# Squares of the sub-norm moved from a PSUM bank to an SBUF tile, and a priority for emptying the banks of transposed probabilities

## The chip, the cores and the metric

The kernel runs on one core of a Trainium2 chip. The metric is the device time of one execution in microseconds (us). The median of the three timed executions of the kernel before is 1237.96 us (1237.94 to 1243.18).

Names used below: PE is TensorE (PEld its weight load), ACT is ScalarE, DVE is VectorE, POOL is GpSimd, SP is the engine whose queue issues most DMAs. L663 is line 663 of the kernel before.

## The reference

Two layers work on 16 meta tokens and 1024 tokens of 1024 features. Each layer computes

```
h = RMSNorm(x)
[f_in | q | k | v | gate] = h @ W_in
Fourier part:   Re(FFT2 over positions and channels) per group, then a 128 x 128 map
Attention part: a = softmax(q0 k0) - lambda * softmax(q1 k1); o = a @ v   (4 heads, two maps each)
                o = RMSNorm(o) * gain                                     (the sub-norm, over the 128 values of a head)
x = x + (concat(Fourier, o) * silu(gate)) @ W_out
```

and the meta tokens are dropped at the end. All of it is float32 to a tolerance that one rounded pass doesn't meet.

## The kernel before

**Split products.** Matmuls take operands rounded to a shorter format (type fp32r). Each operand is split in two: a high part, the rounded copy, and a low part, the value less the high part. A product is then three matmuls (high by high, high by low, low by high). So whatever PE writes to PSUM and later uses as an operand is read out of its bank twice: ACT casts it to the high part, then DVE subtracts that from the bank to get the low part. The bank comes free when DVE is done.

**PSUM.** Three pools divide the eight banks: `big()` is one tile of three banks (S in the profile) for the scores of one softmax map; `gbank()` gives two single banks (G) for projections and output matmuls; `bank()` gives three single banks (M) for transposes and for the attention's products with v.

**Stages of a layer.** `fourier` projects and transforms the Fourier groups. `head_projection` then makes q, k, v and gate of head 0. After that `attention` runs over the 4 heads, in each over four groups of two row tiles of 128 queries, and feeds other work between its own matmuls: `fill` takes steps from the generator `rest`, which holds the projections of heads 1 to 3 (L547 on PE), then the two halves of the output product (L286 on PE).

**One item of attention** (one row tile of one head) is `scores`, then, one item later, `transposes`. In `scores`, for each of the two maps, PE makes 128 x 1040 scores in S (L635, L637), DVE negates them into SBUF and takes the row minimum (L642), ACT takes the exponential with its row sum (L645). DVE then forms the sum's ratio (L649, L651) and subtracts the second map from the first (L653). In `transposes`, PE transposes the resulting p in eight 128 x 128 blocks into two banks of M, four to a bank (L663). ACT copies each bank to `ath` (L667), DVE writes the low part to `atl` (L668). A third bank takes the 16 meta columns (L670), emptied by L673 and L674.

**End of a group.** When the last row tile of a group is transposed, `drain` first calls `flush_finish` for the group before it if that is still open, then `values` multiplies by v into a bank (L682, L683) and copies the result to `osb` (L685). `finish` is called between the next item's scores: SP loads the gate (L693), PE transposes `osb` into a bank of M (L696), ACT copies that back to SBUF (L698). ACT then takes, for each of the two row tiles, the squares of the SBUF copy with their row sum (L703). The squares themselves are not used; before the change they are written over the same bank of M, so the bank stays taken until the second square is done. DVE, POOL and DVE make the scale (L705, L707, L708), DVE applies it (L710), and SP stores the result (L712).

**What sets the order.** The program is traced in the order of the code and each instruction gets a priority from its place. A planner then runs the whole program in a simulated time of its own: on each engine it takes, of the instructions that are ready by that time, the one that comes first in priority; it gives out the buffers of a pool by the same simulated times. What it writes out is a fixed order for each engine with semaphore waits between engines. `tc.high_priority(EVAC)` with EVAC = 600 (L44) puts instructions 600 places ahead; before the change it is used for emptying the G and S banks of the projections (L432, L469) and of the output product (L292). `issue_after` keeps the fed work behind a mark of attention.

**Small tiles.** `sm` (L59) is an SBUF pool of three buffers for each tag. It holds among others `ssq`, `ms`, `rs` of `norm_tile` (L216 to L220), `ss` and `rsq` of the query and key norms (L490, L500), and `r1`, `so`, `rso` of `finish` (L699 to L706).

Of the kernel before, what the change touches and what calls it, by code (L numbers as in the profile page):

```python
# [10 lines left out]
F32 = mybir.dt.float32  # L11
F32R = mybir.dt.float32r
AF = mybir.ActivationFunctionType
ALU = mybir.AluOpType
# [4 lines left out]
P = 128  # L19
# [24 lines left out]
EVAC = 600  # L44
# [6 lines left out]
def trunk(ctx: ExitStack, tc, x, meta, ngain, w_in, w_f, qg, kg, lq1, lk1, lq2, lk2, subg, w_out,  # L51
          ident_d, chan_d, rope_d, dft_d, dftt_d, out, dbg=None):
    nc = tc.nc
    pe, act, dve, pool, sp = nc.tensor, nc.scalar, nc.vector, nc.gpsimd, nc.sync
# [4 lines left out]
    sm = ctx.enter_context(tc.tile_pool(name="sm", bufs=3))  # L59
# [7 lines left out]
    def nm(s):  # L67
        uid[0] += 1
        return f"{s}_{uid[0]}"
# [10 lines left out]
    def f(ap):  # L80
        return ap.bitcast(F32)
# [131 lines left out]
    def norm_tile(hT, hM, gb, xt, t, wk, inplace=False):  # L213
        R, pos = tile_rows(t), P * t
        xn = wk.tile([P, D], F32, tag="xn", name=nm("xn"), bufs=1 if inplace else 2)
        ssq = sm.tile([P, 1], F32, tag="ssq", name=nm("ssq"))  # L216
        act.activation(xn[0:R], xt[0:R], AF.Square, accum_out=ssq[0:R])
        ms = sm.tile([P, 1], F32, tag="ms", name=nm("ms"))
        dve.tensor_scalar(ms[0:R], ssq[0:R], 1.0 / D, EPS, op0=ALU.mult, op1=ALU.add)
        rs = sm.tile([P, 1], F32, tag="rs", name=nm("rs"))  # L220
        pool.tensor_tensor(rs[0:R], ms[0:R], nhalf[0:R, 0:1], op=ALU.pow)
        if inplace:
            xn = xt
        dve.scalar_tensor_tensor(xn[0:R], xt[0:R], rs[0:R], gb[0:R], op0=ALU.mult, op1=ALU.mult)
        for c in range(2):
            pb = bank()
            for j in range(4):
                k = 4 * c + j
                pe.transpose(pb[:, R * j:R * j + R], xn[0:R, P * k:P * k + P], ident[0:R, 0:R])
            src = pb[:, 0:4 * R].rearrange("p (k r) -> p k r", k=4)  # L230
            hi = hT[:, 4 * c:4 * c + 4, 0, pos:pos + R]
            lo = hT[:, 4 * c:4 * c + 4, 1, pos:pos + R]
            act.copy(hi, src)
            dve.tensor_tensor(lo, src, f(hi), op=ALU.subtract)
            if t == NT:
                for o, part in ((0, hi), (32, lo)):
                    act.copy(hM[:, 4 * c:4 * c + 4, o:o + R], f(part))
# [218 lines left out]
    def head_projection(li, h, hT, hM, ep, wk, store, w, nxt, progress):  # L456
        c = P * h
# [6 lines left out]
        ss = None  # L464

        def evacuate(t, ps, a, kv):
            nonlocal ss
            R = tile_rows(t)
            with tc.high_priority(EVAC):  # L469
                if t == NT:  # L470
                    pm = [ep.tile([P, 256], F32, tag="sq", name=nm("pm"), bufs=3) for _ in range(2)]
                    for part, u, v in ((pm[0], a, 256), (pm[1], 256, 384 if kv else 512)):
                        part = part[0:R, u % 256:(v - 1) % 256 + 1]
                        act.copy(part, ps[32:32 + R, u:v])
                        dve.tensor_tensor(part, ps[0:R, u:v], part, op=ALU.add)
                    pqk, pvg = pm[0], pm[1]
                else:
                    pqk, pvg = ps[:, 0:256], ps[:, 256:512]
                if not kv:
                    gs = ep.tile([P, P], F32, tag="gs", name=nm("gs"), bufs=2)  # L480
                    act.activation(gs[0:R], pvg[0:R, P:2 * P], AF.Tanh, scale=0.5)
                    dve.scalar_tensor_tensor(gs[0:R], gs[0:R], 1.0, pvg[0:R, P:2 * P], op0=ALU.add, op1=ALU.mult)
                act.copy(qk[0:R, t, a:256], pqk[0:R, a:256])
                sq = ep.tile([P, 256], F32, tag="sq", name=nm("sq"), bufs=3)
                act.activation(sq[0:R, a:256], pqk[0:R, a:256], AF.Square)
                act.copy(va[0:R, t, :], pvg[0:R, 0:P])
            if not kv:
                sp.dma_start(gtd[li][h][t, 0:R, :], gs[0:R])
            if t % 3 == 0:
                ss = sm.tile([P, 12], F32, tag="ss", name=nm("ss"))  # L490
            c0, c1 = 4 * (t % 3) + a // HD, 4 * (t % 3) + 4
            if t == NT:
                pool.memset(ss[:, 4 * (t % 3):c1], 1.0)
            dve.tensor_reduce(ss[0:R, c0:c1], sq[0:R, a:256].rearrange("p (c d) -> p c d", d=HD), axis=AX.X,
                              op=ALU.add)
            if t % 3 == 2:
                t0 = t - 2
                reg = qk[:, t0:t0 + 3, :]
                dve.tensor_scalar(ss, ss, 1.0 / HD, EPS, op0=ALU.mult, op1=ALU.add)  # L499
                rs = sm.tile([P, 12], F32, tag="rsq", name=nm("rsq"))  # L500
                pool.tensor_tensor(rs, ss, nhalf[:, 0:12], op=ALU.pow)  # L501
                n12 = reg.rearrange("p t (c d) -> p (t c) d", d=HD)
                dve.tensor_tensor(n12, n12, rs.unsqueeze(2).to_broadcast([P, 12, HD]), op=ALU.mult)
                n5 = reg.rearrange("p t (i c d) -> p (t i) c d", i=2, d=HD)

                def tab(x, lo, hi):
                    y = x[:, t0:t0 + 3, :, lo:hi].rearrange("p t i d -> p (t i) d")
                    return y.unsqueeze(2).to_broadcast([P, 6, 2, hi - lo])

                r1 = ep.tile([P, 256], F32, tag="sq", name=nm("r1"), bufs=3)  # L510
                r2 = ep.tile([P, 256], F32, tag="sq", name=nm("r2"), bufs=3)
                r1 = r1[:, 0:12 * ROT].rearrange("p (t c d) -> p t c d", t=6, c=2)
                r2 = r2[:, 0:12 * ROT].rearrange("p (t c d) -> p t c d", t=6, c=2)
                dve.tensor_tensor(r1, n5[:, :, :, 0:ROT], tab(cgt, 0, 16), op=ALU.mult)
                dve.tensor_tensor(r2[:, :, :, 0:8], n5[:, :, :, 8:16], tab(sgt, 0, 8), op=ALU.mult)
                dve.tensor_tensor(r2[:, :, :, 8:16], n5[:, :, :, 0:8], tab(sgt, 8, 16), op=ALU.mult)
                dve.tensor_tensor(n5[:, :, :, 0:ROT], r1, r2, op=ALU.add)
                progress[h] = t // 3 + 1
                if t == NT and ("qk", li, h) in dbg:
                    sp.dma_start(dbg["qk", li, h], qk)  # L520

        for group in [(t,) for t in range(NT - 1)] + [(NT - 1, NT)]:
# [14 lines left out]
            for k in range(KT):  # L537
                for t in group:
# [4 lines left out]
                    else:  # L543
                        hi, lo = hT[:, k, 0, pos:pos + P], hT[:, k, 1, pos:pos + P]
# [11 lines left out]
    def attention(li, wk, store, fill, marks, ready, progress):  # L556
        ath = wk.tile([P, NT, 272], F32R, name="ath", bufs=1)
        atl = wk.tile([P, NT, 272], F32R, name="atl", bufs=1)
# [97 lines left out]
        def transposes(pa, i, t):  # L656
            R = tile_rows(t)
            qo = P * i
            for c in range(2):
                pb = bank()  # L660
                for j in range(4):
                    kt = 4 * c + j
                    pe.transpose(pb[:, R * j:R * j + R], pa[0:R, P * kt:P * kt + P],  # L663
                                 ident[0:R, 0:R])
                src = pb[:, 0:4 * R].rearrange("p (j r) -> p j r", j=4)
                hi = ath[:, 4 * c:4 * c + 4, qo:qo + R]
                act.copy(hi, src)  # L667
                dve.tensor_tensor(atl[:, 4 * c:4 * c + 4, qo:qo + R], src, f(hi), op=ALU.subtract)  # L668
            pb = bank()
            ins = pe.transpose(pb[0:NMETA, 0:R], pa[0:R, SEQ:L], ident[0:R, 0:R])  # L670
            marks.append(ins.ins)
            for o in (0, 64):
                act.copy(att[o:o + NMETA, qo:qo + R], pb[0:NMETA, 0:R])  # L673
            dve.tensor_tensor(att[32:32 + NMETA, qo:qo + R], pb[0:NMETA, 0:R], f(att[0:NMETA, qo:qo + R]),  # L674
                              op=ALU.subtract)
# [12 lines left out]
        def finish(h, gi, osb, ls):  # L688
            sets = [(0, 2, P)] + ([(2, 1, NMETA)] if len(group_tiles(gi)) > 2 else [])
            for i0, n, R in sets:  # L690
# [3 lines left out]
                pb = bank()  # L694
                for i in range(n):
                    pe.transpose(pb[0:R, P * i:P * i + P], osb[:, P * (i0 + i):P * (i0 + i) + R], ident)  # L696
                ot = osb[:, 0:2 * P].rearrange("p (t d) -> p t d", t=2)
                act.copy(ot[0:R, 0:n], pb[0:R, 0:P * n].rearrange("p (t d) -> p t d", t=n))  # L698
                r1 = sm.tile([P, 2], F32, tag="r1", name=nm("r1"))  # L699
                dve.reciprocal(r1[0:R, 0:n], ls[0:R, i0:i0 + n])  # L700
                so = sm.tile([P, 2], F32, tag="so", name=nm("so"))
                for i in range(n):
                    act.activation(pb[0:R, P * i:P * i + P], ot[0:R, i], AF.Square, scale=r1[0:R, i:i + 1],  # L703
                                   accum_out=so[0:R, i:i + 1])
                dve.tensor_scalar(so[0:R, 0:n], so[0:R, 0:n], 1.0 / P, EPS, op0=ALU.mult, op1=ALU.add)  # L705
                rs = sm.tile([P, 2], F32, tag="rso", name=nm("rso"))  # L706
                pool.tensor_tensor(rs[0:R, 0:n], so[0:R, 0:n], nhalf[0:R, 0:n], op=ALU.pow)  # L707
                dve.tensor_tensor(rs[0:R, 0:n], rs[0:R, 0:n], r1[0:R, 0:n], op=ALU.mult)  # L708
                for i in range(n):
# [291 lines left out]
```

## Time and profile before

| | us |
|---|---|
| median of the three timed executions | 1237.96 |
| the profiled execution | 1239.06 |
| its span, from the first instruction to the last | 1236.9 |
| PE busy | 1169.6 |
| DVE busy | 832.9 |
| ACT busy | 647.4 |
| POOL busy | 262.8 |

The profile is of one execution. A row of a timeline reads: start and duration in us, engine, line, operation, what it writes and reads, how many instructions in a row are merged, and in brackets the idle time of the engine before it with what ended it. Matmuls are pipelined, so that a busy PE isn't PE at its peak. By the windows of the profile the first layer's attention lies at about 224 to 630 us, the second layer's at about 860 to 1198 us; the stages between are the Fourier parts, the first head's projections and the ends of the output products.

### The profile page before, as it was taken

How to read it: one execution, taken by the hardware profiler on the slowest of the kernel's cores; microseconds unless marked ns; L12 is line 12 of the kernel's file. 1: busy time of each engine (PE TensorE's matmuls, PEld its weight loads, DVE VectorE, ACT ScalarE, POOL GpSimd, SP SyncE). 2: the span in 40 equal slices, each digit the busy share in tenths (PEclk: the TensorE clock that was granted, in tenths of full speed). 3: DMA queues.
4: the chain of work that ended last, by engine and by line, in shares of the span. 5: the costliest groups of instructions: out<-in, count | busy, mean ns of one | idle time of the engine just before them, and what ended most of it. 6: DMA issues, size and time to landing. Idle time of an engine off the chain costs nothing.

```text
span 1236.9 us, 18756 instructions
## 1 busy us (share of the span) xinstructions
PE 1169.6 (95%) x6676; PEld 1000.8 (81%) x6676; DVE 832.9 (67%) x1793; ACT 647.4 (52%) x1588; POOL 262.8 (21%) x231
## 2 busy tenths in 40 slices
PE   6999899989998998999999999999999999999998
PEld 6999786877777776778879998877878887878786
DVE  6352435777778778887775244557768888898863
ACT  6232325566657667566453323344667666766631
POOL 5111216023212213011012103252142121211200
PEclk9999899999999999999999999999999999999999
DMA  7420203012002004644436111120020020265353
GB/s 227 136 69 35 73 27 99 7 30 75 12 18 82 16 25 147 187 148 130 147 113 197 54 34 55 59 80 26 16 82 22 28 73 25 82 225 162 109 162 114
DMA packets 103612, 105.46 MB, mean 85 GB/s; under 512 B 11232, under 2 KB 87584, under 8 KB 103264
## 3 DMA queue, kind: packets, MB, share of 16 engines
q1 hardware_dynamic: 103104, 99.59, 25.9%
q0 software_dynamic: 416, 4.70, 1.1%
q8 instruction: 52, 0.85, 0.3%
q14 instruction: 40, 0.33, 0.1%
HBM read 74.62 MB, written 29.62 MB: 84 GB/s over the span
## 4 chain that ended last, share of the span: by engine, by line
PE 66%; DVE 12%; DMA 7%; ACT 6%; issue 5%; POOL 2%; SPq 1%; POOLq 0%; ACTq 0%; DVEq 0%
PE G L547 20%; PE G L286 10%; PE G L352 7%; PE S L352 6%; PE M L682 5%; PE S L635 4%; PE S L637 3%; PE S L547 3%; DVE p L642 3%; PE M L663 2%; PE M L393 2%; DMA wst<-in_w_in_dram 2%; ACT p L645 2%; DVE p L653 1%; DMA xt<-in_x_dram 1%
## 5 line engine op out<-in xcount | busy, mean ns | idle before, releaser
L547 PE MATMUL G<-wh,hT 128*128 128x512 f32 x896 | 308.7, 404 | 4.7 <-ACT wh L182 2.5
L645 ACT ACTIVATE p<-p,mx 128x1040 f32<-128x1040 f32 x136 | 158.4, 1165 | 99.7 <-DVE p L642 96.6
L547 PEld LDWEIGHTS G<-wh,hT 128*128 128x128 f32 x896 | 169.2, 190 | 44.6 <-ACT wh L182 3.4
L642 DVE TENSOR_SCALAR_CACHE_REDUCE p<-S 128x1040 f32<-128x1040 f32 x136 | 167.8, 1234 | 33.0 <-PE S L637 28.4
L547 PE MATMUL G<-wl,hT 128*128 128x512 f32 x448 | 178.2, 399 | 1.8 <-POOL wl L184 1.8
L184 POOL TENSOR_TENSOR wl<-wst,wh 128x512 fp32r<-128x512 f32 x82 | 112.6, 1384 | 235.7 <-ACT wh L182 131.1
L286 PE MATMUL G<-wh,yh 128*128 128x512 f32 (+2 forms) x276 | 107.8, 404 | 3.6 <-DVE xt L293 2.3
L182 ACT CAST wh<-wst 128x512 fp32r<-128x512 f32 x128 | 75.0, 620 | 65.0 <-DMA wst<-in_w_in_dram 22.2
L286 PE MATMUL G<-wl,yh 128*128 128x512 f32 (+2 forms) x276 | 106.6, 395 | 0.0
L501 POOL TENSOR_TENSOR rsq<-ss,nhalf 128x12 f32<-128x12 f32 x24 | 58.4, 2433 | 219.4 <-DVE ss L499 190.8
L547 PEld LDWEIGHTS G<-wl,hT 128*128 128x128 f32 x448 | 85.3, 190 | 18.1 <-POOL wl L184 2.8
L352 PE MATMUL G<-hT,wh 128*128 128x384 f32 (+3 forms) x384 | 96.4, 332 | 0.0
L286 PE MATMUL G<-wh,yl 128*128 128x512 f32 (+1 forms) x260 | 93.4, 400 | 0.0
L668 DVE TENSOR_TENSOR atl<-M,ath 128x512 fp32r<-128x512 f32 x136 | 87.0, 656 | 8.0 <-ACT ath L667 6.9
L352 PE MATMUL S<-hT,wh 128*128 128x256 f32 (+3 forms) x384 | 90.7, 320 | 1.0 <-DVE sg L440 1.0
L653 DVE SCALAR_TENSOR_TENSOR p<-p,cc,p 128x1040 f32<-128x1040 f32 (+1 forms) x68 | 89.2, 1312 | 1.5
L637 PE MATMUL S<-k,ql 128*128 128x264 f32 (+3 forms) x408 | 87.3, 321 | 0.0
L667 ACT CAST ath<-M 128x512 fp32r<-128x512 f32 x136 | 73.8, 561 | 22.0 <-PE M L663 21.2
L707 POOL TENSOR_TENSOR rso<-so,nhalf 128x2 f32<-128x2 f32 (+1 forms) x36 | 25.3, 702 | 273.6 <-DVE so L705 256.5
L663 PE MATMUL M<-ident,p 128*128 128x128 f32 x544 | 74.2, 270 | 7.4 <-ACT M L703 3.5
L184 DVE TENSOR_TENSOR wl<-wst,wh 128x512 fp32r<-128x512 f32 x46 | 44.4, 966 | 47.6 <-ACT wh L182 47.3
L663 PEld LDWEIGHTS M<-ident,p 128*128 128x128 f32 x544 | 61.6, 140 | 15.4 <-ACT M L703 4.4
(193 smaller groups left out, 2542.1 us busy)
## 6 DMA issues: line engine op xcount, KB each, us to landing
wst<-in_w_in_dram SPq DMA_DIRECT2D x64, 192.0 KB, 2.8
xt<-in_x_dram SPq DMA_DIRECT2D x16, 512.0 KB, 3.9
wst<-in_w_in_dram SPq DMA_DIRECT2D x32, 256.0 KB, 3.6
wst<-in_w_out_dram SPq DMA_DIRECT2D x16, 512.0 KB, 4.0
xmid<-xt SPq DMA_DIRECT2D x16, 512.0 KB, 3.3
xt<-xmid SPq DMA_DIRECT2D x16, 512.0 KB, 4.3
tab<-in_dft_dram POOLq DMA_DIRECT2D x2, 2096.0 KB, 10.0
yfd<-sg SPq DMA_DIRECT2D x8, 520.0 KB, 2.7
```

What stands on the lines that cost most here:

```text
L182: act.copy(h, self.staged[q][:, j, :])
L184: eng.tensor_tensor(l, self.staged[q][:, j, :], f(h), op=ALU.subtract)
L286: pe.matmul(pb[0:m, 0:e - c], lhsT=a[:, k, 0:m], rhs=b[2 * k + n][:, c:e], start=k == 0 and i == 0, stop=k == 3 and i == n_pass - 1)
L352: pe.matmul(o, lhsT=w[k][:, c:c + P], rhs=hT[:, k, s, a:b], start=k == 0 and i == 0, stop=k == KT - 1 and i == 2)
L547: pe.matmul(pss[t][0:part.shape[-1], a:b], lhsT=part, rhs=w[k][:, a:b], start=k == 0 and i == 0, stop=k == KT - 1 and i == len(pairs) - 1)
L637: ins = pe.matmul(ps[0:R, C0 + a:C0 + b], lhsT=ql[:, qo:qo + R], rhs=kk[:, a:b], start=False, stop=True)
L642: dve.tensor_scalar(pc[0:R], ps[0:R, C0:C0 + L], -1.0, None, op0=ALU.mult, op1=ALU.min, accum_out=mx[0:R])
L645: act.activation(pc[0:R], pc[0:R], AF.Exp, bias=mx[0:R], scale=-1.0, accum_out=lc)
L653: dve.scalar_tensor_tensor(pp[0][0:R], pp[1][0:R], cc[0:R], pp[0][0:R], op0=ALU.mult, op1=ALU.add)
L663: pe.transpose(pb[:, R * j:R * j + R], pa[0:R, P * kt:P * kt + P], ident[0:R, 0:R])
L667: act.copy(hi, src)
L668: dve.tensor_tensor(atl[:, 4 * c:4 * c + 4, qo:qo + R], src, f(hi), op=ALU.subtract)
```

## The change

The squares of `finish` go to a new SBUF tile `sqo` of 128 x 128 with one buffer, in place of the bank of M; their row sums go where they went. L667 and L668 come under `tc.high_priority(EVAC)`. Seven small tags of `sm` get two buffers in place of three.

```diff
@@ norm_tile
-        ssq = sm.tile([P, 1], F32, tag="ssq", name=nm("ssq"))
+        ssq = sm.tile([P, 1], F32, tag="ssq", name=nm("ssq"), bufs=2)
         act.activation(xn[0:R], xt[0:R], AF.Square, accum_out=ssq[0:R])
-        ms = sm.tile([P, 1], F32, tag="ms", name=nm("ms"))
+        ms = sm.tile([P, 1], F32, tag="ms", name=nm("ms"), bufs=2)
         dve.tensor_scalar(ms[0:R], ssq[0:R], 1.0 / D, EPS, op0=ALU.mult, op1=ALU.add)
-        rs = sm.tile([P, 1], F32, tag="rs", name=nm("rs"))
+        rs = sm.tile([P, 1], F32, tag="rs", name=nm("rs"), bufs=2)
@@ head_projection
-                ss = sm.tile([P, 12], F32, tag="ss", name=nm("ss"))
+                ss = sm.tile([P, 12], F32, tag="ss", name=nm("ss"), bufs=2)
...
-                rs = sm.tile([P, 12], F32, tag="rsq", name=nm("rsq"))
+                rs = sm.tile([P, 12], F32, tag="rsq", name=nm("rsq"), bufs=2)
@@ transposes
                 hi = ath[:, 4 * c:4 * c + 4, qo:qo + R]
-                act.copy(hi, src)
-                dve.tensor_tensor(atl[:, 4 * c:4 * c + 4, qo:qo + R], src, f(hi), op=ALU.subtract)
+                with tc.high_priority(EVAC):
+                    act.copy(hi, src)
+                    dve.tensor_tensor(atl[:, 4 * c:4 * c + 4, qo:qo + R], src, f(hi), op=ALU.subtract)
@@ finish
-                so = sm.tile([P, 2], F32, tag="so", name=nm("so"))
+                so = sm.tile([P, 2], F32, tag="so", name=nm("so"), bufs=2)
+                sqo = wk.tile([P, P], F32, tag="sqo", name=nm("sqo"), bufs=1)
                 for i in range(n):
-                    act.activation(pb[0:R, P * i:P * i + P], ot[0:R, i], AF.Square, scale=r1[0:R, i:i + 1],
+                    act.activation(sqo[0:R], ot[0:R, i], AF.Square, scale=r1[0:R, i:i + 1],
                                    accum_out=so[0:R, i:i + 1])
...
-                rs = sm.tile([P, 2], F32, tag="rso", name=nm("rso"))
+                rs = sm.tile([P, 2], F32, tag="rso", name=nm("rso"), bufs=2)
```

## Rows read from the trace of the kernel before

**Rows 1.** The page: span, busy time by engine, the chain by engine.
```profile
span 1236.9 us, 18756 instructions
PE 1169.6 (95%) x6676; PEld 1000.8 (81%) x6676; DVE 832.9 (67%) x1793; ACT 647.4 (52%) x1588; POOL 262.8 (21%) x231
...
PE 66%; DVE 12%; DMA 7%; ACT 6%; issue 5%; POOL 2%; SPq 1%; POOLq 0%; ACTq 0%; DVEq 0%
```

**Rows 2.** Windows, by stage: window, length, PE, PEld, DVE, ACT, POOL, clock, DMA, GB/s.
```profile
224.00:480.00 256.00, 237.81 (x1355) 195.52 (x1354) 200.41 (x452) 165.18 (x413) 54.09 (x45) 0.99 0.13 36
860.00:1085.00 225.00, 218.08 (x1278) 185.59 (x1277) 181.03 (x405) 151.64 (x385) 50.98 (x40) 1.00 0.17 50
480.00:630.00 150.00, 142.36 (x808) 117.29 (x806) 119.41 (x248) 85.71 (x201) 20.38 (x21) 0.99 0.49 154
1085.00:1198.00 113.00, 109.75 (x634) 92.32 (x633) 98.16 (x197) 67.57 (x153) 14.29 (x13) 1.00 0.49 158
```

**Rows 3.** Waits of PE, whole span: released by; us in total, times, longest.
```profile
PE M L670 <- DVE atl L668: 9.5, 6, 3.2
PE M L670 <- ACT M L703: 9.3, 8, 2.0
PE S L635 <- DVE p L642: 4.5, 7, 1.4
PE M L663 <- ACT M L703: 3.5, 3, 1.7
...
PE M L682 <- DVE atl L668: 1.2, 2, 1.0
```

**Rows 4.** Timeline around one wait for the squares: ACT, then PE.
```profile
251.63 0.35 ACT L698 COPY osb<-M 128x256 f32<-128x256 f32 x1
251.89 1.07 ACT L667 CAST ath<-M 128x512 fp32r<-128x512 f32 x2
...
253.38 0.37 ACT L703 ACTIVATE M<-osb,r 128x128 f32<-128x128 f32 x1
...
251.88 0.64 PE L637 MATMUL S<-k,ql 128*128 128x264 f32 x3
253.93 0.28 PE L670 MATMUL M<-ident,p 128*16 128x128 f32 x1 [1.41 <-ACT M L703]
```

**Rows 5.** Timeline around the longest wait for L668, with a finish: ACT, DVE, PE.
```profile
273.48 0.37 ACT L698 COPY osb<-M 128x256 f32<-128x256 f32 x1
...
273.75 2.27 DVE L653 SCALAR_TENSOR_TENSOR p<-p,cc,p 128x1040 f32<-128x1040 f32 x1
276.05 1.29 DVE L668 TENSOR_TENSOR atl<-M,ath 128x512 fp32r<-128x512 f32 x2
...
276.80 0.29 PE L670 MATMUL M<-ident,p 128*16 128x128 f32 x1 [3.17 <-DVE atl L668]
```

**Rows 6.** Timeline around a wait for L668 without a finish: ACT, DVE, PE.
```profile
340.39 1.04 ACT L667 CAST ath<-M 128x512 fp32r<-128x512 f32 x2
...
340.97 1.30 DVE L653 SCALAR_TENSOR_TENSOR p<-p,cc,p 128x1040 f32<-128x1040 f32 x1
342.19 1.28 DVE L668 TENSOR_TENSOR atl<-M,ath 128x512 fp32r<-128x512 f32 x2
...
342.93 0.28 PE L670 MATMUL M<-ident,p 128*16 128x128 f32 x1 [1.80 <-DVE atl L668]
```

**Rows 7.** Single lines: durations in ns, least, median and most; first and last start.
```profile
L703 ACT ACTIVATE M<-osb,r x68: 352/372/421, 252.8 to 1208.3; 128x128 f32<-128x128 f32 x64, 16x128 f32<-16x128 f32 x4
...
L485 ACT ACTIVATE sq<-G x56: 378/391/405, 151.0 to 1075.1; 128x256 f32<-128x256 f32 x56
...
L217 ACT ACTIVATE xn<-xt x18: 1041/1058/1082, 4.5 to 659.6; 128x1024 f32<-128x1024 f32 x16, 16x1024 f32<-16x1024 f32 x2
```

**Rows 8.** Timeline of the first norms: the tightest reuse of a small tile.
```profile
17.32 0.14 DVE L219 TENSOR_SCALAR ms<-ssq 128x1 f32<-128x1 f32 x1
...
21.09 1.06 ACT L217 ACTIVATE xn<-xt 128x1024 f32<-128x1024 f32 x1 [1.91 <-DMA xt<-in_x_dram]
```

## The prediction

> **What bounds the kernel now.** I read the page first: PE is busy for 1169.6 of 1236.9 us and makes 66% of the chain that ended last; DVE follows with 67% busy and 12% of the chain [rows 1]. So a microsecond counts if PE stands still in it. The windows then say where PE stands still [rows 2]. In the first layer's attention it is idle for 256.0 - 237.8 = 18.2 us (7.1%) and 150.0 - 142.4 = 7.6 us (5.1%); in the second layer's, which runs the same code, for 6.9 us of 225 (3.1%) and 3.3 us of 113 (2.9%). The granted clock is 0.99 or 1.00 of full speed in all four, the higher of the two levels, so it plays no part here.
>
> The waits of PE name what ended those idle times [rows 3]. The single transpose of the meta columns, L670, waits 9.3 us in 8 waits for the squares L703, and 9.5 us in 6 waits for the low parts L668. The block transposes L663 wait 3.5 us in 3 waits for L703, and the product with v waits 1.2 us for L668. All these want a bank of M. By comparison PE waits just 4.5 us for the bank of scores, which L642 empties.
>
> The timelines show how one such wait arises. In [rows 4] PE is done with the second scores at 251.88 + 0.64 = 252.52 and next in its fixed order stands L670. The three banks of M are held by the two blocks of transposes and by the group's finish. ACT had copied the finish's bank out by 251.98, yet the bank stays taken until the second square ends at 253.75, and PE sits for 1.41 us. Behind L670 in PE's queue stand matmuls of the projections that need nothing of M: all of it is delayed.
>
> **The squares.** They are still computed, at the same place in ACT's code; only their bank is let go, at the end of L698. For the wait of [rows 4] this would mean 251.98 in place of 253.75, ahead of PE's arrival, so the wait goes entirely. There are eleven waits of this kind, 9.3 + 3.5 = 12.8 us [rows 3]; in the eleven timelines L698 ends before PE arrives, or within 0.2 us of it. Term A: 12.8 us.
>
> Some waits for L668 have the same root. In [rows 5] L670 gets the bank of L668 at 276.80 after 3.17 us, though L698 had copied the finish's bank by 273.85: with that bank free at once, L670 needs no other. I count four such waits at L670 (at 276.80, 355.45, 454.87 and 905.58), 3.17 + 0.73 + 0.73 + 1.24 = 5.9 us. Term B: 5.9 us.
>
> What a square costs ACT can change with its target. SBUF to PSUM, 128 columns, takes 372 ns [rows 7]; no row has a 128-column square from SBUF to SBUF. From below: L217, SBUF to SBUF, takes 1058 ns for 1024 columns, and L485, PSUM to SBUF, 391 ns for 256, so 667 ns for 768 columns, 0.87 ns each, and 1058 - 896 x 0.87 = 0.28 us. From above: the 391 ns of L485 with twice the columns. I take 0.37, being nearest to the same instruction; the ends give -6 and +1 us over 68 squares, on an engine that is 62 to 67% busy in these windows [rows 2], and PE no longer waits for them. At PE: nothing.
>
> The Trainium skill speaks against this edit: "ScalarE: Activation LUTs", section "Step-by-step: what each stage is for", says that an ACTIVATE writes faster to PSUM than to SBUF, with the reservation that it is of use only where TensorE doesn't need most of PSUM. By the rule each square gets slower by an amount that the section doesn't give; by the waits of PE, the reservation is this kernel's case.
>
> **The priority.** L667 and L668 (136 of each) now go ahead of whatever else is ready: on ACT past the exponential L645, the copy L698, the squares and the weight casts; on DVE past L642, L653, the norm work and the key and query low parts. No DMA is issued by either line, so SP's and POOL's queues are not passed; finish's scale on POOL and the store after it move by as much as L698 does. Two effects count.
>
> For: in [rows 6] there is no finish. ACT has the first of the two banks cast at about 340.9 (half of 1.04 after 340.39), but DVE begins the 1.30 us of L653 at 340.97 and L668 only at 342.19; PE waits 1.80 us. L668 first would give the bank 1.30 us sooner. There are two such waits (342.93 and 442.35). Term C: 2 x 1.3 = 2.6 us; its lower end is 0, if the planner sees L653 ready first, as it may have been here, within 0.1 us.
>
> Against: L698 does not come under the priority. In [rows 4] the two L667 (1.07 us together) would go before L698 where both are ready, and the finish's bank is let go at about 251.98 + 1.0 = 253.0, after PE's arrival at 252.52. So about 0.5 us of the wait stays. I apply this to the 11 + 4 events of A and B: 15 x 0.5 = 7.5 us given back (0 if the planner keeps L698 ahead, 15 us if the pair is always ahead and each wait keeps 1 us).
>
> **The small tiles.** With two buffers a norm's square waits for the scale of two tiles before. The tightest place is the start, where nothing covers it: the square at 21.09 would need the L219 that ended at 17.46, 3.6 us before [rows 8]. In the head projections and finishes a tag comes round once in tens of us. I cost this at 0; if it were late, ACT's queue behind L217 would be held in the first 45 us. The `sqo` buffer is written by ACT alone, whose order serves.
>
> **The sum.** 12.8 + 5.9 + 2.6 - 7.5 = 13.8, say 14 us. A second way: were the first layer's attention idle only as often as the second's, it would save 18.2 - 0.031 x 256 = 10.3 and 7.6 - 0.029 x 150 = 3.3 us, 13.6 together. The profiled execution took 1239.06 us, 1.1 above the median: 1239.06 - 14 = 1225.1, on the median's scale 1224.0 us.
>
> **The rivals.**
>
> *More of it is kept.* The planner keeps L698 ahead and the second layer gains as well: A + B + C = 21.3 and most of the 1.2 and 4.5 us for the product and the scores. Time 1238 - 24 = 1214. For it: none of these waits is bound to a busy engine. Against: a planner's times were wrong in all of them, and will be elsewhere. Chance 0.14.
>
> *The two parts cancel, or DVE is next.* The pair of L667 delays L698 in every finish, so each event keeps 1 us (21.3 - 15 = 6.3), and a few waits for DVE grow: DVE is already busy for 78, 80, 80 and 87% of the four windows [rows 2]. Time about 1238 - 3 = 1235. For it: L698 is late in [rows 4, 5] because ACT is behind, and L667 makes it later. Against: the second layer runs at 80% DVE with just 3% of PE idle. Chance 0.25.
>
> *The priority holds up the scores.* S is one buffer: PE's next scores wait for L642. Two L668 (1.28 us, [rows 5, 6] have such pairs) now stand before an L642 that was first. PE waits 4.5 us for S now, so there is mostly slack; but if the 1.28 us reaches PE in 17 of the 68 items (17 x 1.28 = 21.8) the gain of 21.3 is gone, in 22 it is slower by over 0.5%, and in 25 it costs 32, net +11: 1249 us. For it: DVE at 87% in the last window. Against: an item takes about 406 / 36 = 11 us in the first layer and needs S only twice. Chance 0.14.
>
> **How the numbers follow.** The forecast's case has the remaining 0.47. A measurement of this kernel can tell 0.5% (6.2 us) from no change. Faster by more: forecast and larger gain, 0.47 + 0.14 = 0.61. Within 0.5%: 0.25. Slower by more: 0.14. The range: its low end is the whole of the waits in [rows 3] named above, 9.5 + 9.3 + 3.5 + 1.2 + 4.5 = 28, thus 1210, less 3 for shifts in the order, 1207. The high end takes in the second rival and half of the slower one: 1244. For the forecast's own case, 1216 to 1231.
>
> **What would show it.** In the profile after: no wait of PE for L703 (now 12.8 us); L670's wait for L668 under 4 us (now 9.5); a new, small wait of L670 or L663 for L698 (7 us by my sum); squares of about 0.37 us; the first layer's windows idle for about 3 to 4% of their length. Against me: L635's wait for L642 above 10 us, or L670 waiting 10 us or more for L698, or a time above 1232 us.

## The result and the profile after

The changed kernel takes 1221.01 us (median of four executions, 1219.41 to 1223.81) against 1239.51 us (median of four) for the kernel before. The ratio is 0.9856 with a 95% interval of 0.9837 to 0.9875: faster by 1.4%. The profiled execution took 1222.14 us, 16.9 us less than the one read before. Of all executions of the kernels below, one, the fourth of the change's repetition, took 1906.07 us; it stands in no median and no ratio here.

The page of the kernel after, in the lines that answer to [rows 1]:

```profile
span 1220.4 us, 18764 instructions
PE 1166.7 (96%) x6676; PEld 1001.9 (82%) x6676; DVE 835.6 (68%) x1793; ACT 644.8 (53%) x1588; POOL 264.3 (22%) x231
...
PE 66%; DVE 13%; DMA 6%; ACT 5%; issue 5%; POOL 3%; SPq 1%; POOLq 0%; DVEq 0%; ACTq 0%
```

The engines do the same work in a shorter span. PE's idle time over the whole span falls from 67.3 to 53.7 us, which is 13.6 of the 16.5 us that the span is shorter; the other 2.9 us are PE's busy time. The windows of the kernel after, as in [rows 2]:

```profile
224.00:480.00 256.00, 245.84 (x1408) 203.28 (x1407) 208.65 (x475) 173.85 (x437) 55.57 (x46) 0.99 0.15 44
480.00:630.00 150.00, 145.30 (x823) 119.43 (x822) 119.91 (x245) 84.76 (x195) 19.70 (x22) 0.99 0.48 156
860.00:1085.00 225.00, 218.53 (x1275) 185.43 (x1273) 190.28 (x412) 151.13 (x381) 56.36 (x42) 1.00 0.21 62
```

In the first layer PE is now idle for 10.2 us of 256 (18.2 before) and 4.7 of 150 (7.6 before); in the second for 6.5 of 225 (6.9 before). These windows have the bounds of [rows 2], though in the shorter kernel the work lies earlier. With bounds that move with the work, each layer's attention reads so, the kernel before in the first pair, the kernel after in the second:

```profile
224.00:630.00 406.00, 380.17 (x2161) 312.81 (x2160) 319.82 (x699) 250.89 (x613) 74.47 (x66) 0.99 0.26 80
860.00:1198.00 338.00, 327.82 (x1910) 277.91 (x1909) 279.19 (x601) 219.21 (x537) 65.27 (x53) 1.00 0.28 86
```

```profile
224.00:613.00 389.00, 376.03 (x2154) 311.81 (x2153) 315.88 (x699) 249.69 (x613) 73.67 (x64) 1.00 0.27 83
845.00:1184.00 339.00, 330.11 (x1922) 280.73 (x1921) 285.08 (x602) 218.61 (x538) 67.87 (x53) 1.00 0.28 86
```

PE's idle time falls from 25.8 to 13.0 us in the first layer's attention and from 10.2 to 8.9 in the second's. The gain lies in the first layer: the exponential of the first layer's last item starts 15.6 us earlier than before, and all that follows adds 1 us.

The waits of PE after the change, whole span. The priority adds a line, so L671 is the old L670, L669 the old L668, L683 the old L682 and L699 the old L698; the squares are L705:

```profile
PE M L671 <- DVE atl L669: 6.6, 6, 1.4
PE S L635 <- DVE p L642: 3.8, 6, 0.9
...
PE M L683 <- DVE atl L669: 0.8, 1, 0.8
...
PE M L663 <- ACT osb L699: 0.5, 2, 0.2
...
PE M L671 <- ACT osb L699: 0.2, 1, 0.2
```

Against [rows 3]: no wait for the squares at all (12.8 us before), 6.6 us for the low parts in place of 9.5, and 0.7 us for the finish's copy. All waits of PE ahead of matmuls into banks of M in attention (a few of them for an operand) add up to 30.0 us before and 12.8 us after, 17.2 us less. That this lies close to the 16.9 us of the profiled executions is in part chance: PE's whole idle time fell by 13.6 us alone, so some 3.6 us came back at other waits, such as L229's for L234 (0.7 us before, 2.5 after) and L547's for L486 (1.3 before, 2.6 after), and 2.9 us came off PE's busy time.

The place of [rows 4] in the kernel after, ACT, then PE:

```profile
252.05 0.35 ACT L699 COPY osb<-M 128x256 f32<-128x256 f32 x1
252.30 1.08 ACT L668 CAST ath<-M 128x512 fp32r<-128x512 f32 x2
253.26 0.42 ACT L705 ACTIVATE sqo<-osb,r 128x128 f32<-128x128 f32 x1
...
252.30 0.63 PE L637 MATMUL S<-k,ql 128*128 128x264 f32 x3
252.77 0.27 PE L671 MATMUL M<-ident,p 128*16 128x128 f32 x1
252.80 0.71 PE L547 MATMUL G<-wh,hT 128*128 128x512 f32 x2
```

ACT does the same things in the same order up to the first square (copy, two casts, square), but PE takes the finish's bank at 252.77, after the copy that ended at 252.40 and ahead of the squares. The projections behind L671 follow at once. In the kernel before they came later:

```profile
253.96 0.48 PE L547 MATMUL G<-wh,hT 128*128 128x512 f32 x1
```

The second scores start 0.42 us later than before (252.30 against 251.88), the projections behind the wait 1.16 us earlier (252.80 against 253.96). Up to here each engine has its instructions in the order of the kernel before (PE's order first differs at 258 us of the kernel before). So these 1.6 us come from letting the bank go, and not from a new plan.

### The profile page after: what moved, and what is told of

Its sections match the earlier page's. It is cut to its first block, busy times and chain, and to the rows that moved or that the text cites. A ratio compares the mean times of both kernels' runs of the same rounds, so it can differ in the third digit from the quotient of the medians.

```text
span 1220.4 us, 18764 instructions
## 1 busy us (share of the span) xinstructions
PE 1166.7 (96%) x6676; PEld 1001.9 (82%) x6676; DVE 835.6 (68%) x1793; ACT 644.8 (53%) x1588; POOL 264.3 (22%) x231
## 4 chain that ended last, share of the span: by engine, by line
PE 66%; DVE 13%; DMA 6%; ACT 5%; issue 5%; POOL 3%; SPq 1%; POOLq 0%; DVEq 0%; ACTq 0%
PE G L547 19%; PE G L286 10%; PE G L352 7%; PE M L683 6%; PE S L352 6%; PE S L635 4%; PE S L637 4%; PE S L547 3%; DVE p L642 3%; PE M L663 2%; PE M L393 2%; DMA wst<-in_w_in_dram 2%; POOL wl L184 2%; DVE p L653 2%; DMA xt<-in_x_dram 2%
## 5 line engine op out<-in xcount | busy, mean ns | idle before, releaser
L547 PE MATMUL G<-wh,hT 128*128 128x512 f32 x896 | 306.6, 401 | 6.0 <-ACT va L486 2.6
L547 PEld LDWEIGHTS G<-wh,hT 128*128 128x128 f32 x896 | 168.2, 189 | 46.1 <-ACT va L486 3.9
L642 DVE TENSOR_SCALAR_CACHE_REDUCE p<-S 128x1040 f32<-128x1040 f32 x136 | 167.6, 1232 | 29.3 <-PE S L637 22.8
L547 PE MATMUL G<-wl,hT 128*128 128x512 f32 x448 | 177.2, 398 | 1.8 <-POOL wl L184 1.7
L547 PEld LDWEIGHTS G<-wl,hT 128*128 128x128 f32 x448 | 84.7, 189 | 18.1 <-POOL wl L184 2.9
L501 POOL TENSOR_TENSOR rsq<-ss,nhalf 128x12 f32<-128x12 f32 x24 | 55.0, 2293 | 203.6 <-DVE ss L499 182.5
L653 DVE SCALAR_TENSOR_TENSOR p<-p,cc,p 128x1040 f32<-128x1040 f32 (+1 forms) x68 | 90.2, 1327 | 1.5
L669 DVE TENSOR_TENSOR atl<-M,ath 128x512 fp32r<-128x512 f32 x136 | 86.3, 655 | 6.7 <-ACT ath L668 5.8
L637 PE MATMUL S<-k,ql 128*128 128x264 f32 (+3 forms) x408 | 87.0, 321 | 0.0
L668 ACT CAST ath<-M 128x512 fp32r<-128x512 f32 x136 | 72.6, 562 | 15.2 <-PE M L663 14.6
L663 PE MATMUL M<-ident,p 128*128 128x128 f32 x544 | 73.0, 270 | 2.3 <-DVE p L653 0.9
L683 PE MATMUL M<-ath,vh 128*128 128x256 f32 (+1 forms) x256 | 73.2, 286 | 0.8 <-DVE atl L669 0.8
```

What stands on the lines that cost most here:

```text
L547: pe.matmul(pss[t][0:part.shape[-1], a:b], lhsT=part, rhs=w[k][:, a:b], start=k == 0 and i == 0, stop=k == KT - 1 and i == len(pairs) - 1)
L637: ins = pe.matmul(ps[0:R, C0 + a:C0 + b], lhsT=ql[:, qo:qo + R], rhs=kk[:, a:b], start=False, stop=True)
L642: dve.tensor_scalar(pc[0:R], ps[0:R, C0:C0 + L], -1.0, None, op0=ALU.mult, op1=ALU.min, accum_out=mx[0:R])
L653: dve.scalar_tensor_tensor(pp[0][0:R], pp[1][0:R], cc[0:R], pp[0][0:R], op0=ALU.mult, op1=ALU.add)
L683: pe.matmul(po[:, 0:w], lhsT=v[:, kt, :], rhs=a[:, kt, 0:w], start=kt == 0 and i == 0, stop=False)
```

## The experiments

The theory: PE waited for the finish's bank, held by squares that nobody reads; letting it go is the gain. Its rivals: the priority makes the gain; the place where the squares are written does; a new plan shifts the time by chance. Lines are those of each run's own kernel. Where a kernel is said to have the same order as another, each engine's instructions stand in the same order in the two traces. The kernels ran on several chips, so each is compared with the kernel before on its own chip.

**The squares alone.** The change without the priority.

```diff
-                with tc.high_priority(EVAC):
-                    act.copy(hi, src)
-                    dve.tensor_tensor(atl[:, 4 * c:4 * c + 4, qo:qo + R], src, f(hi), op=ALU.subtract)
+                act.copy(hi, src)
+                dve.tensor_tensor(atl[:, 4 * c:4 * c + 4, qo:qo + R], src, f(hi), op=ALU.subtract)
```

> The squares go to SBUF, with the small tiles at two buffers, and L667 and L668 keep their old place in the order. If the finish's bank is what PE waited for (main theory), most of the gain is here: by terms A and B 12.8 + 5.9 us come off and nothing is given back, so 13 to 19 us below before, no wait of PE for L703, and the waits without a finish (L670 for L668, two of 1.8 us) stay. If the priority made the gain, this is within 5 us of before.

Measured: 1219.02 us against 1237.23, ratio 0.9835 (0.9808 to 0.9862). The whole gain is here. No wait for the squares is left, and the waits for the low parts and for the scores are those of the change:

```profile
PE M L670 <- DVE atl L668: 6.6, 6, 1.4
PE S L635 <- DVE p L642: 3.8, 6, 0.9
```

One point of the expectation missed: the two waits of 1.8 us without a finish did not stay. The plan made for this kernel has its waits in other places. The run was repeated:

> The squares alone once more, beside the run before and against a second set of runs of before. Main theory: 16 to 20 us below before, so that the priority of the change is worth nothing within 2 us either way.

Measured: 1222.01 us against 1239.50, ratio 0.9860 (0.9843 to 0.9876).

**The priority alone.** Squares and small tiles as before.

```diff
-                act.copy(hi, src)
-                dve.tensor_tensor(atl[:, 4 * c:4 * c + 4, qo:qo + R], src, f(hi), op=ALU.subtract)
+                with tc.high_priority(EVAC):
+                    act.copy(hi, src)
+                    dve.tensor_tensor(atl[:, 4 * c:4 * c + 4, qo:qo + R], src, f(hi), op=ALU.subtract)
```

> L667 and L668 under the priority, squares still over the bank of M, small tiles as before. Main theory: term C alone, at most 2.6 us, and since L698 and the squares now stand behind the two casts, the bank is held longer: waits of PE for L703 grow from 12.8 to 15 us or more; time between 3 us below and 8 us above before. If the priority made the gain: 8 us or more below before.

Measured: 1240.60 us against 1237.23, ratio 1.0022 (1.0005 to 1.0039). The priority makes none of the gain; alone it costs 0.2%. The waits of PE in this run (L704 are the squares):

```profile
PE M L671 <- ACT M L704: 9.9, 8, 1.6
PE M L671 <- DVE atl L669: 9.6, 7, 3.2
...
PE M L663 <- ACT M L704: 4.0, 3, 1.7
```

The waits for the squares grow from 12.8 to 13.9 us, less than the 15 I expected, and nothing of term C shows in the waits for the low parts (9.6 us, 9.5 before).

**The small tiles alone.** Seven tags at two buffers, `bufs=2` as in the diff of the change, nothing else.

> Only the seven small tags at two buffers, nothing else changed. Main theory: no change, within 2 us of before, the same waits of PE for L703 (12.8 us) and L668 (9.5 us). If a mere new plan moves the time by chance as much as the change did, this is off by 5 us or more in either direction.

Measured: 1237.46 us against 1237.23, ratio 0.9993 (0.9978 to 1.0009). The order of the instructions on all five engines is the same as before: the planner had no use for the third buffers. The edit is free. As it made no new plan, this run does not test the third rival.

**The bank held.** The whole change, and a copy of one column that keeps the finish's bank taken until the squares are done.

```diff
                     act.activation(sqo[0:R], ot[0:R, i], AF.Square, scale=r1[0:R, i:i + 1],
                                    accum_out=so[0:R, i:i + 1])
+                act.copy(sqo[0:R, 0:1], pb[0:R, 0:1])
```

> The whole change, and behind the two squares a one-column copy from the finish's bank, so that the bank is taken as long as before though the squares go to SBUF. It adds 36 copies of about 0.2 us on ACT. Main theory (the bank's hold costs, not where the squares are written): 10 to 16 us slower than the change, about 1231 to 1237 us, with PE waiting 9 us or more for this copy. If the target of the squares or the priority made the gain: within 4 us of the change, 1217 to 1225 us.

Measured: 1247.60 us against 1237.23, ratio 1.0066 (1.0039 to 1.0092). The gain is gone, as the theory has it, with eleven waits of this kind, as many as before, now for the copy (L707):

```profile
PE M L671 <- DVE atl L669: 10.5, 8, 1.8
PE M L671 <- ACT sqo L707: 8.4, 8, 2.2
PE S L635 <- DVE p L642: 5.3, 6, 1.5
PE G L788 <- DMA ya<-yad: 4.8, 1, 4.8
PE M L663 <- ACT sqo L707: 4.4, 3, 1.9
```

But it lies some 10 us above the kernel before, where I expected it at 1231 to 1237. One wait for a DMA, 4.8 us in the profiled execution and 0.9 before, has a part in it. Otherwise either the priority, or the copy with its plan, costs that. Two more runs tell these apart. The first is the squares alone with the same copy, so without the priority:

> The squares alone, with the one-column copy behind them that keeps the finish's bank taken (36 copies of 0.16 us on ACT), and the casts in their old place. If the hold alone undoes the gain and the bank-held run stood 10 us above before because of the priority: within 4 us of before. If the copy itself, or the plan made for it, cost that: 6 us or more above before, as with the priority. If the target of the squares were the gain: within 4 us of the squares alone.

Measured: 1246.16 us against 1238.60, ratio 1.0057 (1.0040 to 1.0074). So it isn't the priority. The second is the kernel before with the copy, the squares still over their bank:

```diff
                     act.activation(pb[0:R, P * i:P * i + P], ot[0:R, i], AF.Square, scale=r1[0:R, i:i + 1],
                                    accum_out=so[0:R, i:i + 1])
+                cb = sm.tile([P, 1], F32, tag="cb", name=nm("cb"), bufs=1)
+                act.copy(cb[0:R], pb[0:R, 0:1])
```

> The kernel before with the same 36 copies behind the squares, which stay over their bank; the seven small tags at two buffers. It holds the bank as long as the run before this one and differs from it only in where the squares are written. Both theories of the hold: the same time as that run within 2 us. Against before: 0 to 4 us more, if the cost is that the bank is held 0.2 us longer per finish (11 waits, 2 us); 6 us or more, if the new plan costs.

Measured: 1245.60 us against 1238.60, ratio 1.0059 (1.0036 to 1.0081), the same as the run before it. This pair is the cleanest of the study. The two kernels have the same order on all five engines and hold the bank equally long (2.0 us from the end of the finish's copy to the end of the one-column copy, medians of 36); they differ in where the squares are written, and the time is the same. So with the bank held, moving the squares to SBUF is worth nothing; without the hold it is worth 17.5 to 18.2 us. How much of that is the release of the bank and how much the plan that comes with it stays open, beyond the one place shown above. A plan can matter: the copies, 36 of 0.16 us, with the plan made for them, cost 7 us. In this run the waits for banks of M add up to 35.4 us (30.0 before), those for S in attention to 6.9 (5.1). Its largest ones:

```profile
PE M L670 <- DVE atl L668: 10.4, 8, 1.8
PE M L670 <- ACT cb L706: 7.5, 7, 2.2
PE S L635 <- DVE p L642: 5.7, 6, 1.4
PE M L663 <- ACT cb L706: 4.6, 3, 1.9
PE M L682 <- DVE atl L668: 3.7, 2, 2.7
```

**More priority.** Four runs on one chip. First the change again:

> The changed kernel as it is, beside the three that follow. Main theory (the squares alone make the gain, the priority is nearly idle): the same 16 to 20 us below before as the squares alone. If the priority costs or gains on top of the squares, it stands 3 us or more off the 18.2 us that the squares alone gave.

Measured: 1220.09 us against 1238.82, ratio 0.9853 (0.9831 to 0.9875). Beside the squares alone (0.9835 and 0.9860), the priority is worth nothing that can be measured. The orders show why: with and without it, PE's order is the same for the first 3148 of its 6676 matmuls and differs in 13 places in all, ACT's in 18 of 1588 and DVE's in 38 of 1793. Next, the finish's copy first too:

```diff
-                act.copy(ot[0:R, 0:n], pb[0:R, 0:P * n].rearrange("p (t d) -> p t d", t=n))
+                with tc.high_priority(EVAC):
+                    act.copy(ot[0:R, 0:n], pb[0:R, 0:P * n].rearrange("p (t d) -> p t d", t=n))
```

> The change, and the finish's copy L698 under the priority too. My give-back step (the casts go ahead of L698, which holds the finish's bank 0.5 us per wait): 4 to 7 us below the change. Rival, that L698 was never pushed behind the casts: within 2 us of the change, and the waits of L670 for L668 (6.6 us) stay as they are.

Measured: 1219.57 us, ratio 0.9848 (0.9832 to 0.9864): no change, and the wait for L668 stays at 6.6 us. The order on all five engines is that of the change. In the trace the casts stand between a finish's transposes and its copy in 3 of 36 finishes, with the priority and without. Nothing had pushed the copy back. Next, everything that empties a bank of M in attention; the diff shows the meta columns, and the same stands around L590 to L592, L620 to L622, L685 and L698:

```diff
-            for o in (0, 64):
-                act.copy(att[o:o + NMETA, qo:qo + R], pb[0:NMETA, 0:R])
+            with tc.high_priority(EVAC):
+                for o in (0, 64):
+                    act.copy(att[o:o + NMETA, qo:qo + R], pb[0:NMETA, 0:R])
...
```

> The change, and everything that empties a bank of M in attention under the priority (finish's copy, meta columns, product with v, keys, queries). If the remaining waits for banks (about 12 us in the trace after) come from the order on ACT and DVE: 4 to 8 us below the change. If they come from DVE being behind the plan, whatever comes first: within 3 us of the change either way, with the sum of the waits on M between 9 and 15 us.

Measured: 1225.71 us, ratio 0.9892 (0.9876 to 0.9909), 5.6 us slower than the change. The waits on M stay (14.2 us against 14.0 in the change's profile of the same chip), and PE waits longer for the scores' bank and for the queries (L637 is the old L635, L644 the old L642):

```profile
PE S L637 <- DVE p L644: 5.8, 8, 1.5
...
PE S L637 <- DVE qa L623: 2.4, 2, 1.7
```

So the banks of M did not come free earlier for being emptied first, and the bank of scores came free later. Last, L642 under the priority too:

> As the run before, with the emptying of the scores (L642) under the priority too. If the priority of the casts holds up the scores (third rival of the prediction): the wait of L635 for L642 falls from 3.8 us to under 2 and the time is 2 us or more below the run before. If it doesn't: within 2 us of it.

Measured: 1224.35 us, ratio 0.9894 (0.9874 to 0.9913), the same as the run before it; the wait of L635 for L642 is 4.2 us, less than the 5.8 us of the run before it, but not under the 3.8 us of the change.

**One finish at a time.** Three of the six waits of L670 for the low parts in the squares alone stand at ends of groups with three row tiles (in the first layer a head's last group also holds the meta tokens), where `finish` runs twice in a row. This kernel puts the second one an item later (on the squares alone).

```diff
-                fin[0] = (h, gi, osb, sums[h, gi])
+                sets = [(0, 2, P)] + ([(2, 1, NMETA)] if len(tiles) > 2 else [])
+                fin.extend((h, gi, osb, sums[h, gi], [part]) for part in sets)
...
-                        (lambda: (fill(2), flush_finish()), lambda: fill(2)))
+                        (lambda: (fill(2), flush_finish(1)), lambda: fill(2)))
```

> The squares alone, and in the groups of three row tiles (four in the first layer) the finish of the meta tile comes one item later, so that a group's end takes one bank of M at a time and not two. If the waits that stayed at those group ends (L663 for the finish's copy 0.4 us, then L670 for L668 1.3 us, three times) come from two finishes in a row: 3 to 5 us below the squares alone, about 1214 to 1216 us, and those three pairs of waits gone. If they come from ACT and DVE being behind in any case: within 2 us of the squares alone, with new waits in the same places.

Measured: 1224.51 us, ratio 0.9879 (0.9861 to 0.9898): 2.5 us above the squares alone on the same chip (1222.01), where I expected 3 to 5 below. The intervals of the two ratios overlap, so slower isn't shown, but a gain of 3 us is ruled out. The three pairs of waits are gone, but two waits of 2.7 us stand an item later, one of them here, DVE, then PE:

```profile
334.34 0.48 DVE L622 SCALAR_TENSOR_TENSOR ql<-M,qgc,qa 64x256 fp32r<-64x256 f32 x1
334.74 1.28 DVE L653 SCALAR_TENSOR_TENSOR p<-p,cc,p 128x1040 f32<-128x1040 f32 x1
335.95 1.27 DVE L668 TENSOR_TENSOR atl<-M,ath 128x512 fp32r<-128x512 f32 x2
...
336.68 0.28 PE L670 MATMUL M<-ident,p 128*16 128x128 f32 x1 [2.74 <-DVE atl L668]
```

The low parts come after the queries' work and L653 on DVE. Whether the priority would have helped in this kernel was not tried.

## Why the prediction was right, and where it was not

The forecast was 1224.0 us within 1207 to 1244, from a sum of 14 us. Measured, it was 18.5 us between the medians and 16.9 between the profiled executions. The bound was read rightly: PE's idle time in the first layer's attention, ended by the squares and the low parts.

**Term A (12.8 us).** The 9.3 us of L670 came as worked out: its eight waits for L703 are gone. The 3.5 us of L663 did not come. At the ends of groups with three tiles, where those three waits stood, L663 now waits 0.5 us in two waits for the copy, and then L671 waits 1.13, 1.13 and 0.85 us for the low part. One of the three, in the kernel after, ACT, then PE:

```profile
326.89 0.37 ACT L699 COPY osb<-M 128x256 f32<-128x256 f32 x1
327.36 0.40 ACT L705 ACTIVATE sqo<-osb,r 128x128 f32<-128x128 f32 x1
...
327.76 0.56 ACT L668 CAST ath<-M 128x512 fp32r<-128x512 f32 x1
...
327.32 0.66 PE L663 MATMUL M<-ident,p 128*128 128x128 f32 x4 [0.24 <-ACT osb L699]
329.10 0.28 PE L671 MATMUL M<-ident,p 128*16 128x128 f32 x1 [1.13 <-DVE atl L669]
```

A square still stands ahead of the cast on ACT, as in the squares alone, though L663's first four transposes were done at 327.08 (326.48 + 0.60). I had not asked what the next bank after the freed one would wait for.

**Term B (5.9 us).** It came: in the first layer the wait of 3.17 us in [rows 5] is 0.17 us for the copy in the kernel after, those at 355 and 455 are gone, and at 905 L670's is gone while L663 still waits 0.8 us for a low part. But three new waits for low parts, of 0.76, 1.37 and 1.38 us, stand at 261.99, 473.92 and 1033.81, where none of the six old ones stood. They and the three of term A are the 6.6 us.

**Term C (2.6 us).** Its two waits of 1.8 us are gone, but by the plan that came with the squares (they are gone in the squares alone too) and not by the priority: with that alone the four waits for low parts between 335 and 460 us still add up to 5.1 us, as before, and the time is 0.2% longer. Here the reading of the mechanism failed. The prediction let the casts go "ahead of whatever else is ready"; the planner decides only between instructions that are ready in its own simulated time, and with the squares moved the priority changed 18 of 1588 places on ACT.

**The give-back (7.5 us)** is the step that failed most: "the two L667 would go before L698 where both are ready". They don't: casts stand between a finish's transposes and its copy in 3 of 36 finishes before and after, PE waits 0.7 us for the copy, and putting it first changed nothing. C and the give-back together made -4.9 us; measured, the priority is worth about 0. With A and B alone, 18.7 us less 3.5, the sum would have been 15.2. That the sum of 14 came so near is in part luck: a give-back that did not come stood in for the new waits for low parts, which no term had, and for what came back at other waits.

**The second way** of the sum, the second layer's idle share, gave 13.6 us. The first layer's windows came to 4.0% and 3.1%, against 3.1% and 2.9% read from the second; with the moved bounds it is 13.0 of 389 us, 3.3%.

**The squares' price** was bounded by 0.28 and 0.39 us and taken at 0.37. It is 0.404, above the upper bound, which was read from another instruction. (The 62 to 67% for ACT in that passage should be 57 to 67%, by [rows 2].)

```profile
L705 ACT ACTIVATE sqo<-osb,r x68: 387/404/448, 253.3 to 1191.8; 128x128 f32<-128x128 f32 x64, 16x128 f32<-16x128 f32 x4
```

That is 32 ns more for each than with PSUM as the target [rows 7], 2.2 us of ACT over 68. The Trainium skill ("ScalarE: Activation LUTs", "Step-by-step: what each stage is for") says that ScalarE writes faster to PSUM: the trace agrees. In the time of the kernel it can't be seen: the pair of held runs differs by 0.6 us, and in the kernel after no wait of PE ends at a square.

**The small tiles** cost 0, as predicted, though in the finishes a tag does not always come round "once in tens of us": at the four ends of groups with three tiles L705 of the kernel before comes again after 2.5 to 6.4 us. **The rivals:** the priority did not hold up the scores (L635 waits 3.8 us, 4.5 before), and the two parts did not cancel. DVE is at 82, 80 and 85% of the three fixed windows above, and most of what PE still waits for in attention is DVE's (L669 with 6.6 us, L642 with 3.8), but not enough to take the gain away. My bar for the waits for low parts, under 4 us, was missed at 6.6.

## What to carry to other kernels

A scratch result that nobody reads still holds the buffer it is written to: look at what keeps a scarce PSUM bank taken after its last useful read, and compare that end with the arrival of the engine that wants the bank. When an engine's order is fixed, a wait of one small instruction (here sixteen columns of a transpose) delays all that stands behind it, so count such waits by who ended them before costing a change. And a sum of waits isn't yet a gain: here 17.2 us of waits at these banks went and PE's whole idle time fell by 13.6. A priority is worth testing by itself: here it changed few places of the order, and given to all that empties a bank of M it made the kernel 0.4% slower.

## What was not expected of the hardware

The granted clock falls to its lower level after some of PE's waits, though the means of the windows hide it. Stretches of the kernel before, and of the kernel after (window, length, PE, PEld, DVE, ACT, POOL, clock, DMA, GB/s):

```profile
270.00:276.90 6.90, 3.73 (x25) 2.65 (x23) 5.55 (x8) 5.57 (x13) 3.75 (x3) 1.00 0.25 71
276.90:280.30 3.40, 3.40 (x9) 1.99 (x9) 2.72 (x8) 0.70 (x3) 0.69 (x1) 0.51 0.05 9
280.30:290.00 9.70, 9.70 (x64) 8.25 (x63) 6.05 (x12) 8.48 (x19) 6.28 (x5) 1.00 0.50 143
```

```profile
467.00:475.50 8.50, 6.14 (x36) 4.73 (x36) 8.37 (x18) 8.39 (x22) 3.71 (x4) 1.00 0.57 183
475.50:478.90 3.40, 3.40 (x18) 3.40 (x17) 3.30 (x9) 2.70 (x7) 0.00 (x0) 0.50 0.64 150
```

In the kernel before, PE was idle for 3.17 us up to 276.80 [rows 5], and from 276.90 the granted clock was 0.51 for 3.4 us, the 1.2 GHz level, with PE busy throughout. In the kernel after, the same place has no such wait and no dip; one stands at 475.5, behind 2.4 us of idle time in 8.5. In that dip L683 starts every 0.21 us (476.13, 476.35, 476.56), behind it every 0.12 (479.04, 479.16, 479.28). So 3.4 us hold about half the work, and by my estimate a dip adds some 1.7 us to a wait that seemed to cost only itself. Not every such wait brings one: three of 1.80 to 1.82 us in the kernel before, at 342.9, 376.3 and 442.4, did not.

The prediction said that the clock plays no part, and that was wrong. Within the first layer's attention there are two dips before, at 276.9 and 573.9, and one after, at 475.5 (the next, at 618.9, lies behind it). Over the whole span but its last microsecond the clock was at the lower level for 20.5 us before and 17.1 us after, so by the same estimate 1.7 of the 16.5 us between the spans are the clock's. They need not be the change's: dips also differ between executions of one order. Between 224 and 800 us the profile of the squares alone has one (at 376.6) and a span of 1215.0 us, its repetition three (474.5, 617.9, 754.4) and 1220.2 us.
